# A projection taken two tiles at a time around a chunk batch and the last head's turn, and an output projection whose pools open while retention still holds its own

## The chip, the cores and the metric

The kernel runs on one NeuronCore of a Trainium2 chip. The core's engines run side by side, each in the order its own instruction stream was written in: TensorE (PE in the profile; its weight loads are the row PEld), VectorE (DVE), ScalarE (ACT), GpSimd (POOL) and SyncE (SP), which mostly issues DMAs. A DMA issue that has to wait for its source holds back every later one on the same issuing engine. The metric is device time in microseconds; smaller is better.

## The reference

One layer of a hybrid diffusion backbone over 1024 latent tokens and a 256-token context prefix, width 1024, float32. Cut to what matters here:

```python
p = (h @ w_in)                                    # h: modulated RMSNorm of [context ; latent], 1280 tokens
qkv_a, z, ab, rq, rk, rv, rg = split(p)           # 4 delta-rule heads, 4 retention heads, 128 wide
q, k, v = short_conv(qkv_a)                       # centred, 5 taps, SiLU; q and k are L2-normalised
A   = strict_lower((k*beta) @ k.T * decay)        # per chunk
sol = triangular_solve(A + I, [v*beta, k*beta*exp(G)])
o_gdn = scan over chunks, forward and backward    # state S per head
o_gdn = rms_norm(o_f + o_b) * silu(z)
o_ret = head_group_norm(r_f + r_b) * silu(rg)     # retention, forward and backward
x = x + g1 * (concat(o_gdn, o_ret)[latent] @ w_out)
x = x + g2 * swiglu(modulate(rms_norm(x)), w_ffn_in, w_ffn_out)
return rms_norm(x, final_g)
```

The change touches the z columns of `p`, the building of `A` for the last chunks, and the seam between retention and the product with `w_out`.

## The kernel before, in words

Tokens are taken in ten tiles of 128: tiles 0 and 1 are the context, 2 to 9 the latents. Large products are computed in three fp32r matmuls (high weights by high activations, low by high, high by low), so every weight appears as `whi` and `wlo`, every activation as `hhi` and `hlo`.

Program order around the first part of the change:

- `conv_block` projects one head of q, k or v and convolves it; `vturn(h)` transposes head h of v token by token on TensorE (`vT`, L855), scales it on ScalarE (`vt`, L858) and stores it (L859).
- `pre(t)` prepares tile t for the triangular solve: `kk` (L705), `qt` (L710, its squares summed by ScalarE at L712), `kq` (L715); then for both directions an affine mask on GpSimd (`e`, L722), exponentials on ScalarE (L726), `ut` on VectorE (L730) stored to DRAM as `un` (L734), and `sp` (L733, L737) stored as `sd` (L738).
- The tiles go in three batches, `BATCH = [[0,1,2,9],[3,8,4,7],[5,6]]`, called b0, b1 and b2 below. `invert` solves a batch's 32x32 diagonal blocks on VectorE: it loads them (`X<-un` and `yr<-un`, L753), copies (L756), runs 30 pairs of multiply and subtract (`tmp`, L766; `X`, L770), transposes (`XT`, L774) and stores (`xd`, L776). `merge` puts the blocks together by small matmuls (`m`, L812 to L839), reading `U` and `t` that L788 to L793 load from `un` and `xd`.
- `token_major(g, tiles)` multiplies all tiles by one 256-column group of `w_in`. It takes the tiles in pairs, two PSUM banks at a time; a tile has 24 matmuls (`tm`, L371 to L373), and `tm_store` empties its bank into `res` (for z a SiLU on ScalarE, L532) and stores it (L387). For z, `res` has two buffers. Groups 8 and 9 are z.
- The order written out is: v's convolutions with `vturn(0)` to `vturn(2)`; z's group 8, all eight latent tiles; `vturn(3)`; `pre(5)` and `pre(6)`; `merge(0)`; `invert(1, 2)`, one run of 30 steps over both batches; `merge(1)`, `merge(2)`; z's group 9; then the two-way scan and retention.

Retention's forward pass over the last four tiles is `forward_tail`: transposes of q and k (`rqT`, `rkT`, L1065 and L1066), scores (`rP`, L1079) masked into `pm` (L1081), the output (`ro`, L1088 to L1090), then a group norm (copy `oc` L1092, statistics L1096 and L1098, scaling on ScalarE L1103, gate on GpSimd L1106) and a store to the DRAM tensor `dy` (L1107). The delta rule's half of `dy` is stored by `gate` as `dy<-yo` (L971, L973). After it the pools of retention and scan close, and the output projection begins: `wo_half` prepares half of `w_out` (load `woraw` L1172, high part L1177, low part L1178); `op_y(l)` loads a token tile of `dy` (`yt`), transposes it (`yT`, L1194) and splits it (`yhi` L1197, `ylo` L1198); `op_mm` does the 24 matmuls of one tile and one half of the columns (`op`, L1208 to L1210). The second half of `w_out`'s low and high parts is written partly into the tiles of pool `h2` (`b11`, `t2` and so on), which lies where retention's pool RT lay.

The order of the instructions on each engine isn't that of the source alone: a list scheduler with a simulated timeline picks, at each moment, among the operations whose inputs it expects to be ready, and program order decides between them. Pools matter to it too, since a tile can only be written once the tile that had its space is done with.

Of the kernel before, what the change touches and what calls it, by code (L numbers as in the profile page):

```python
# [8 lines left out]
F32 = mybir.dt.float32  # L9
# [8 lines left out]
P = 128  # L18
# [20 lines left out]
def build(nc, tc, ap, dbg=None, stop=None, marks=None):  # L39
# [151 lines left out]
    try:  # L191
# [187 lines left out]
        def tm_store(g, t, o, finish, store, pl):  # L379
            early = g < 2  # L380
            res = (W2 if early else R1).tile([P, 256], F32, tag="res", name="res", bufs=4 if early else 2)
            finish(t, o[:, 0:256], res)
            if g == 0:
                S.activation(xa[:, t, :], o[:, 256:WIDE], AF.Copy)
            nm, c0 = GROUPS[g // 2], (g % 2) * 256
            dst = zd[t - 2, :, c0:c0 + 256] if nm == "z" else rd[t, :, RD[nm], c0:c0 + 256]
            store.dma_start(dst, res)  # L387

        def token_major(g, tiles, finish, store, pl, q=S):

            w = [tm_weights(g, kh, pl, q) for kh in range(2)]

            for p in range(0, len(tiles), 2):
                pair = [(t, tm_bank(g)) for t in tiles[p:p + 2]]
                for kh in range(2):
                    for t, o in pair:
                        tm_half(o, w[kh], kh, t)
                for t, o in pair:
                    tm_store(g, t, o, finish, store, pl)

        def fin_copy(t, o, res):
# [460 lines left out]
        for h in range(H):  # L862
            vys.append(newy())
            conv_block(8 + h, vys[h], False)
            if h:
                vturn(h - 1, vys[h - 1])
        token_major(8, LAT, fin_gate, S, W)
        vturn(H - 1, vys[H - 1])
        close(CV)
        checkpoint("v")  # L870
        RP = pool("rp", side="right")
        rope = RP.tile([P, TT, P], F32, tag="rope", name="rope")
        GM = pool("gm", side="right")
        for t in BATCH[2]:
            pre(t)
        close(GP)
# [238 lines left out]
        def forward_tail(ts, cur):  # L1115


            nxt = turn(ts[0], True)
            for t in ts:
                kk, vv, gt, qk = nxt  # L1120
                state = cur
                if t < TT - 1:
                    nxt = turn(t + 1, True)
                    cur = rstate(0, kk, vv, cur, "Rf")
                output(t, vv, gt, qk, scores(qk, True), state, True)

        TAIL = 4
        work = [(backward, t) for t in [1, 0] + list(range(TT - 1, 1, -1))] + [(forward, t) for t in range(TT - TAIL)]
        cur = None
        for s, n in enumerate((0,0,3,3,3,2,2,2,1,0)):  # L1130
# [4 lines left out]
            work = work[n:]  # L1135
        forward_tail(range(TT - TAIL, TT), cur)
        checkpoint("scan")
        close(RT)
        close(PK)
        close(SC)  # L1140
        close(RP)
        close(GS)

        H2 = pool("h2")
        X = {n: H2.tile([P, 2, 4, 4, P], F32R, tag=n, name=n) for n in ("b11", "t2", "t1", "t3", "b21", "t4", "b22")}  # L1150

        def xhi(n, q, k=slice(0, 4)):
            return X[n][:, 0, q, k, :]

        def xlo(n, q, k=slice(0, 4)):
            return X[n][:, 1, q, k, :]

        OR = pool("or", side="right")
# [5 lines left out]
        S.dma_start(gain, ap["gains"])  # L1164
        slabs = [X[n][:, i, 3].rearrange("p k t -> p (k t)") for n in X for i in range(2)]

# [13 lines left out]

        wo = [wo_half(n) for n in range(2)]
        dx1 = dr.tile([LT, P, D], F32, tag="dx1", name="dx1")
        SY.dma_start(g1r, grow[0][0].partition_broadcast(P))
        banks(pa=3, pb=2, pc=3)

# [17 lines left out]
        def op_mm(y, n):  # L1203
# [8 lines left out]
            V.tensor_tensor(x1[:, ns], x1[:, ns], xl[:, ns], ALU.add)  # L1212

        held = {}

# [46 lines left out]
        before = None  # L1262
        pairs = (1, 5, 2, 6, 0, 4, 3, 7)
        nxt = op_y(pairs[0])
        for i, l in enumerate(pairs):
            y = nxt
            if l != 7:
                nxt = op_y(pairs[i + 1])
            op_mm(y, int(l == 7))
            if before:  # L1270
# [391 lines left out]
```

## Time and profile before

| what | value |
|---|---|
| time, median of three runs (lowest, highest) | 1473.67 us (1473.1, 1477.56) |
| the profiled execution's own time | 1475.05 us |
| its span, first to last instruction | 1473.3 us |
| mean granted TensorE clock | 0.981 |
| PE busy | 1400.1 us, 95% of the span |
| DVE, ACT, POOL busy | 962.7, 614.1, 592.0 us |
| instructions in the span | 24112 |
| z group 8 to the end of `merge(2)` | 361.6 to about 491 us |
| scan and retention | about 491 to 711 us |
| output projection | from 712.9 us |
| feed-forward | from about 820 us |

TensorE is busy through most of the program. A row of the timeline gives the start, the duration, the engine, the line, the operation with what it writes and reads, and in brackets the idle time ahead of it with what ended it. A view of windows gives each engine's busy time in a stretch, with the clock granted to TensorE and the share of time that the DMA engines were busy.

### The profile page before, as it was taken

Reading aid. Unit: us, or ns where it says so; the run is one execution under the profiler, and the core shown is the slowest. Engines: PE = TensorE matmul, PEld = TensorE weight load, DVE = VectorE, ACT = ScalarE, POOL = GpSimd, SP = SyncE. Lnnn points to the kernel's source line nnn. Section 1 sums busy time; section 2 is a strip of 40 time slices with the busy share of each in tenths; the row PEclk is TensorE's granted clock in tenths of the full one; section 3 lists DMA queues with packets and bytes.
Section 4 is the critical chain, followed back from the end, with each engine's and each line's share of the span. In section 5 each row is a group of like instructions: output and inputs, shape, how many; then the busy total and the mean of one; then the engine's idle time right before and its main releaser. Section 6 shows DMA issues by size and latency. Waiting matters only on the chain.

```text
span 1473.3 us, 24112 instructions
## 1 busy us (share of the span) xinstructions
PE 1400.1 (95%) x8919; PEld 1202.5 (82%) x8919; DVE 962.7 (65%) x1853; ACT 614.1 (42%) x1325; POOL 592.0 (40%) x495
## 2 busy tenths in 40 slices
PE   7999999988879999899799899999999999999997
PEld 2798888978878999898688688877888888788886
DVE  6566789279665344689677877656555564657577
ACT  5553554578522211245443623223333332454445
POOL 0120001144103334244144688898555553335322
PEclk9999999999989999999899999999999999999999
DMA  9536586688797744996533265774222242786863
GB/s 330 190 98 227 175 254 211 196 257 262 224 260 213 286 155 155 414 367 203 191 121 108 91 238 210 248 259 160 103 107 107 107 151 79 239 283 193 296 211 115
DMA packets 170549, 298.14 MB, mean 202 GB/s; under 512 B 43624, under 2 KB 94008, under 8 KB 166080
## 3 DMA queue, kind: packets, MB, share of 16 engines
q1 hardware_dynamic: 118880, 253.17, 50.2%
q10 hardware_dynamic: 49072, 35.83, 7.8%
q0 software_dynamic: 2480, 7.60, 1.4%
q8 instruction: 70, 1.15, 0.3%
q14 instruction: 47, 0.39, 0.1%
HBM read 206.60 MB, written 89.96 MB: 201 GB/s over the span
## 4 chain that ended last, share of the span: by engine, by line
PE 44%; POOL 6%; DVE 3%; DMA 3%; issue 2%; ACT 2%; ACTq 0%; POOLq 0%; DVEq 0%
PE ffn L1351 7%; PE ffn L1350 6%; PE ffn L1349 6%; PE fo L1477 4%; PE fo L1475 4%; PE fo L1476 4%; DMA wd<-tw 2%; PE op L1208 2%; PE op L1209 2%; PE op L1210 2%; POOL ws L1322 1%; POOL tw L1403 1%; POOL tw L1402 1%; POOL tw L1405 1%; PE ru L1032 1%
## 5 line engine op out<-in xcount | busy, mean ns | idle before, releaser
L371 PE MATMUL tm<-whi,hhi 128*128 128x256 f32 (+1 forms) x704 | 201.4, 290 | 11.3 <-ACT res L532 5.3
L372 PE MATMUL tm<-wlo,hhi 128*128 128x256 f32 (+1 forms) x704 | 200.8, 287 | 2.1 <-DVE wlo L345 2.1
L373 PE MATMUL tm<-whi,hlo 128*128 128x256 f32 (+1 forms) x704 | 199.0, 287 | 0.0
L371 PEld LDWEIGHTS tm<-whi,hhi 128*128 128x128 f32 x704 | 134.4, 192 | 14.6 <-ACT res L532 5.7
L372 PEld LDWEIGHTS tm<-wlo,hhi 128*128 128x128 f32 x704 | 135.2, 192 | 4.8 <-DVE wlo L345 2.5
L1349 PE MATMUL ffn<-t,whi 128*128 128x512 f32 x352 | 137.0, 390 | 1.9 <-ACT whi L344 1.9
L1351 PE MATMUL ffn<-t,wlo 128*128 128x512 f32 x352 | 137.0, 390 | 1.2 <-DVE wlo L345 1.2
L1350 PE MATMUL ffn<-t,whi 128*128 128x512 f32 x352 | 137.0, 389 | 0.0
L373 PEld LDWEIGHTS tm<-whi,hlo 128*128 128x128 f32 x704 | 134.4, 192 | 0.8 <-DVE hlo L314 0.2
L344 ACT ACTIVATE whi<-wraw 128x512 fp32r<-128x512 f32 (+2 forms) x98 | 75.2, 771 | 135.7 <-PE ffn L1350 82.7
L344 ACT ACTIVATE whi<-ws 128x512 fp32r<-128x512 f32 x88 | 55.6, 632 | 170.5 <-PE ffn L1350 123.1
L345 DVE TENSOR_TENSOR wlo<-ws,whi 128x512 fp32r<-128x512 f32 x88 | 96.0, 1091 | 44.3 <-ACT whi L344 44.1
L1475 PE MATMUL fo<-whi,ahi 128*128 128x512 f32 x308 | 119.3, 390 | 0.9 <-ACT ahi L344 0.9
L1476 PE MATMUL fo<-wlo,ahi 128*128 128x512 f32 x308 | 120.0, 390 | 0.0
L1477 PE MATMUL fo<-whi,alo 128*128 128x512 f32 x308 | 119.0, 390 | 0.0
L345 DVE TENSOR_TENSOR wlo<-wraw,whi 128x512 fp32r<-128x512 f32 (+2 forms) x92 | 101.7, 1107 | 20.1 <-ACT whi L344 20.0
L1349 PE MATMUL ffn<-b,whi 128*128 128x512 f32 x264 | 103.7, 393 | 4.5 <-ACT whi L344 4.5
L1351 PE MATMUL ffn<-b,wlo 128*128 128x512 f32 x264 | 103.5, 392 | 1.1 <-DVE wlo L345 1.1
L1350 PE MATMUL ffn<-b,whi 128*128 128x512 f32 x264 | 103.4, 392 | 0.0
L611 PE MATMUL b<-hhi,whi 128*128 128x512 f32 (+1 forms) x256 | 95.2, 372 | 0.9 <-ACT y L615 0.9
L613 PE MATMUL b<-hhi,wlo 128*128 128x512 f32 (+1 forms) x256 | 94.8, 370 | 0.0
L612 PE MATMUL b<-hlo,whi 128*128 128x512 f32 (+1 forms) x256 | 94.4, 369 | 0.0
(444 smaller groups left out, 3440.7 us busy)
## 6 DMA issues: line engine op xcount, KB each, us to landing
adaw<-ada SPq DMA_DIRECT2D x48, 512.0 KB, 5.0
pk<-sd SPq DMA_DIRECT2D x16, 1536.0 KB, 13.7
wraw<-wfi SPq DMA_DIRECT2D x44, 512.0 KB, 3.5
ar<-ad SPq DMA_DIRECT2D x33, 512.0 KB, 5.8
w<-wfo SPq DMA_DIRECT2D x22, 512.0 KB, 4.4
wd<-tw SPq DMA_DIRECT2D x11, 1024.0 KB, 4.9
ad<-act SPq DMA_DIRECT2D x20, 512.0 KB, 2.8
raw<-wd SPq DMA_DIRECT2D x20, 512.0 KB, 4.9
```

Of the source, the lines that this page charges most:

```text
L344: S.activation(hi, raw, AF.Copy)
L345: e.tensor_tensor(lo, raw, hi.bitcast(F32), ALU.subtract)
L371: T.matmul(o, hhi[:, k, tsl], whi[:, k % 4, :], start=(k == 0), stop=False)
L372: T.matmul(o, hhi[:, k, tsl], wlo[:, k % 4, :], start=False, stop=False)
L373: T.matmul(o, hlo[:, k, tsl], whi[:, k % 4, :], start=False, stop=(k == KT - 1))
L611: T.matmul(o, whi[:, k, :], hh, start=(k == 0), stop=False)
L1349: T.matmul(o, whi[:, k, :], xhi(xn, slice(0, 4), k), start=(first and k == 0), stop=False, **kw)
L1350: T.matmul(o, whi[:, k, :], xlo(xn, slice(0, 4), k), start=False, stop=False, **kw)
L1351: T.matmul(o, wlo[:, k, :], xhi(xn, slice(0, 4), k), start=False, stop=(k == 3), **kw)
L1475: T.matmul(po[g][i], ahi[:, ts], whi, start=(j == 0 and not kw), stop=False, **kw)
L1476: T.matmul(po[g][i], ahi[:, ts], wlo, start=False, stop=False, **kw)
L1477: T.matmul(po[g][i], alo[:, ts], whi, start=False, stop=(j == FH - 1), **kw)
```

## The change

Every engine keeps its number of instructions; what changes is their order, one buffer count and the order in which pools open and close.

- `res` gets four buffers for every group.
- `token_major` becomes a loop over a generator, `token_pairs`, that yields after each pair of tiles. Group 8 of z now runs thus: `pre(5)` and `pre(6)` first in program order, then two pairs, then `vturn(3)`, then the other two pairs.
- `forward_tail` becomes a generator that yields after each tile. The scan's and retention's other pools close, and the output projection's pools open, ahead of it; retention's pool RT closes behind it. After the tail's first tile come `wo_half(0)` and `op_y` of token tile 1, after its third the first half `op_mm` of that tile. Pool `h2`, the second half of `w_out` and the new PSUM bank tags come after the tail.

```diff
-            res = (W2 if early else R1).tile([P, 256], F32, tag="res", name="res", bufs=4 if early else 2)
+            res = (W2 if early else R1).tile([P, 256], F32, tag="res", name="res", bufs=4)
...
         def token_major(g, tiles, finish, store, pl, q=S):
 
+            for _ in token_pairs(g, tiles, finish, store, pl, q):
+                pass
+
+        def token_pairs(g, tiles, finish, store, pl, q=S):
+
             w = [tm_weights(g, kh, pl, q) for kh in range(2)]
-
             for p in range(0, len(tiles), 2):
                 pair = [(t, tm_bank(g)) for t in tiles[p:p + 2]]
...
                 for t, o in pair:
                     tm_store(g, t, o, finish, store, pl)
+                yield
...
-        token_major(8, LAT, fin_gate, S, W)
+        for t in BATCH[2]:
+            pre(t)
+        z8 = token_pairs(8, LAT, fin_gate, S, W)
+        next(z8)
+        next(z8)
         vturn(H - 1, vys[H - 1])
+        for _ in z8:
+            pass
...
-        for t in BATCH[2]:
-            pre(t)
         close(GP)
...
                 output(t, vv, gt, qk, scores(qk, True), state, True)
+                yield
...
-        forward_tail(range(TT - TAIL, TT), cur)
         checkpoint("scan")
-        close(RT)
         close(PK)
         close(SC)
         close(RP)
         close(GS)
...
-        wo = [wo_half(n) for n in range(2)]
+        wo = []
...
+        pairs = (1, 5, 2, 6, 0, 4, 3, 7)
+        tail = forward_tail(range(TT - TAIL, TT), cur)
+        next(tail)
+        wo.append(wo_half(0))
+        nxt = op_y(pairs[0])
+        next(tail)
+        next(tail)
+        op_mm(nxt, 0)
+        for _ in tail:
+            pass
+        close(RT)
+        H2 = pool("h2")
...
+        slabs = [X[n][:, i, 3].rearrange("p k t -> p (k t)") for n in X for i in range(2)]
+
+        wo.append(wo_half(1))
+        banks(pa=3, pb=2, pc=3)
...
-        pairs = (1, 5, 2, 6, 0, 4, 3, 7)
-        nxt = op_y(pairs[0])
         for i, l in enumerate(pairs):
             y = nxt
             if l != 7:
                 nxt = op_y(pairs[i + 1])
-            op_mm(y, int(l == 7))
+            if i:
+                op_mm(y, int(l == 7))
```

How that moves the instructions is read from the order on an engine. The first place is TensorE at the end of z's group 8, where b2's second tile (6) is prepared. Before, all 192 `tm` matmuls of group 8 come first:

```order
L372 MATMUL tm<-wlo,hhi 128x256
L373 MATMUL tm<-whi,hlo 128x256
L855 MATMUL vT<-ident,y 128x128 x2
L705 MATMUL kk<-kc 128x128 x4
L710 MATMUL qt<-ident,qc 128x128 x2
L855 MATMUL vT<-ident,y 128x128 x4
L710 MATMUL qt<-ident,qc 128x128 x2
L715 MATMUL kq<-qc,kc 128x128 x4
L855 MATMUL vT<-ident,y 128x128 x4
```

In the change the same `kk` and `qt` (now L710 and L715) stand behind 56 of them; `kq` follows 8 `tm` later, and the ten `vT` of the last head after 32 more:

```order
L371 MATMUL tm<-whi,hhi 128x256
L372 MATMUL tm<-wlo,hhi 128x256
L710 MATMUL kk<-kc 128x128 x4
L715 MATMUL qt<-ident,qc 128x128 x4
L373 MATMUL tm<-whi,hlo 128x256
```

So tile 6's preparation moved ahead of 136 `tm` matmuls. On SP, which issues the loads and stores of the solve, the piece from b0's last store on was, before (`un_2892`, `un_2893` and `un_2894` are the `un` of b0, b1 and b2; `xd_3181` is b0's):

```order
L776 DMA xd_3181<-XT 64x1024
L753 DMA X<-un_2893 16x32x32 x4
L734 DMA un_2894<-ut 128x512 x2
L753 DMA yr<-un_2894 8x32x32
L738 DMA sd<-sp 128x1024 x2
L753 DMA X<-un_2894 8x32x32 x4
L753 DMA yr<-un_2894 8x32x32
L788 DMA U_4298<-un_2892 128x4096
L880 DMA rope<-rope 128x1280
L793 DMA t_4300<-xd_3181 32x32x32 x4
```

and is now:

```order
L739 DMA un_2894<-ut 128x512
L758 DMA yr<-un_2894 8x32x32
L743 DMA sd<-sp 128x1024
L781 DMA xd_3181<-X 64x1024
L781 DMA xd_3181<-XT 64x1024
L781 DMA xd_3181<-X 64x1024
L781 DMA xd_3181<-XT 64x1024
L758 DMA X<-un_2893 16x32x32 x4
L793 DMA U_4298<-un_2892 128x4096
L889 DMA rope<-rope 128x1280
L758 DMA X<-un_2894 8x32x32
L798 DMA t_4300<-xd_3181 32x32x32 x4
```

b2's stores of `ut` moved ahead of b0's stores of the solved blocks and of b1's `X` loads. On VectorE the second `ut` of tile 6 likewise stands within the last steps of b0's solve, ahead of `tmp` with 84 columns.

The second place is TensorE at the end of retention. Before, the transposes `yT` come behind the output `ro` of the last tile, and 24 `op` follow:

```order
L1089 MATMUL ro<-Rb_6925,qk 128x128
L1090 MATMUL ro<-vg,pm 128x128
L1088 MATMUL ro<-Rf,qk 128x128
L1089 MATMUL ro<-Rb_6925,qk 128x128
L1090 MATMUL ro<-vg,pm 128x128
L1194 MATMUL yT<-ident,yt 128x128 x8
```

In the change they stand behind `ro` of tile 7, and everything of tiles 8 and 9 from the transposes of q and k on stands behind them, mixed with the 24 `op`:

```order
L1098 MATMUL ro<-Rb_7031,qk 128x128
L1099 MATMUL ro<-vg,pm 128x128
L1186 MATMUL yT<-ident,yt 128x128 x8
L1074 MATMUL rqT<-ident,kq 128x128 x4
L1075 MATMUL rkT<-ident,kq 128x128 x4
L1074 MATMUL rqT<-ident,kq 128x128 x4
L1075 MATMUL rkT<-ident,kq 128x128 x4
L1088 MATMUL rP<-qk 128x128 x4
L1097 MATMUL ro<-Rf,qk 128x128
L1200 MATMUL op<-wohi,yhi 128x512
L1201 MATMUL op<-wolo,yhi 128x512
```

The first `yt` still stands right behind the last `dy<-yo` on SP. Before:

```order
L1172 DMA woraw<-wo 128x512
L664 DMA vg<-rd 128x1024
L1172 DMA woraw<-wo 128x512 x3
L973 DMA dy<-yo 128x512
L664 DMA yt<-dy 128x512 x2
L664 DMA xl<-x 128x1024 x2
```

In the change, where only the loads ahead of it are in another order:

```order
L669 DMA vg<-rd 128x1024
L982 DMA dy<-yo 128x512
L1165 DMA woraw<-wo 128x512 x4
L982 DMA dy<-yo 128x512
L669 DMA yt<-dy 128x512 x2
L669 DMA xl<-x 128x1024 x2
```

From the feed-forward on, the order on TensorE is the same as before.

More of the change, by code (lines that the diff above doesn't have):

```diff
@@ L1142, in build @@
         close(GS)
[L1149 to L1156, printed above, removed]
         OR = pool("or", side="right")
@@ L1164, in build @@
         S.dma_start(gain, ap["gains"])
-        slabs = [X[n][:, i, 3].rearrange("p k t -> p (k t)") for n in X for i in range(2)]
+        slabs = []
         def wo_half(n):
@@ L1179, in wo_half @@
             return hi, lo
-        wo = [wo_half(n) for n in range(2)]
+        wo = []
         dx1 = dr.tile([LT, P, D], F32, tag="dx1", name="dx1")
         SY.dma_start(g1r, grow[0][0].partition_broadcast(P))
-        banks(pa=3, pb=2, pc=3)
         def op_y(l):
@@ L1212, in op_mm, with xhi, xlo @@
             V.tensor_tensor(x1[:, ns], x1[:, ns], xl[:, ns], ALU.add)
+        pairs = (1, 5, 2, 6, 0, 4, 3, 7)
[10 more added lines that the diff above has]
+        H2 = pool("h2")
+        X = {n: H2.tile([P, 2, 4, 4, P], F32R, tag=n, name=n) for n in ("b11", "t2", "t1", "t3", "b21", "t4", "b22")}
+        def xhi(n, q, k=slice(0, 4)):
+            return X[n][:, 0, q, k, :]
+        def xlo(n, q, k=slice(0, 4)):
+            return X[n][:, 1, q, k, :]
+        slabs = [X[n][:, i, 3].rearrange("p k t -> p (k t)") for n in X for i in range(2)]
+        wo.append(wo_half(1))
+        banks(pa=3, pb=2, pc=3)
         held = {}
```

## The prediction, on record before the result was seen

> **What bounds the kernel now.** I read the page's busy times first, then windows cut at the stages the change touches, then TensorE's waits in them, then the timelines of the engines it waits for.
>
> ```profile
> PE 1400.1 (95%) x8919; PEld 1202.5 (82%) x8919; DVE 962.7 (65%) x1853; ACT 614.1 (42%) x1325; POOL 592.0 (40%) x495
> ...
> 360.00:400.00 40.00, 33.10 (x266) 32.69 (x267) 27.86 (x56) 24.62 (x68) 10.26 (x8) 0.96 0.76 211
> 400.00:460.00 60.00, 47.92 (x1019) 45.64 (x1018) 44.46 (x124) 11.08 (x20) 9.71 (x14) 0.88 0.89 249
> 460.00:490.00 30.00, 30.00 (x493) 28.60 (x492) 9.81 (x24) 9.58 (x18) 10.09 (x18) 0.95 0.73 238
> 490.00:580.00 90.00, 90.00 (x795) 89.80 (x794) 36.69 (x118) 10.10 (x15) 37.08 (x77) 1.00 0.49 176
> 580.00:690.00 110.00, 103.81 (x902) 101.71 (x901) 86.86 (x333) 43.65 (x136) 40.32 (x37) 1.00 0.88 336
> 690.00:730.00 40.00, 29.48 (x161) 25.05 (x161) 29.93 (x97) 22.87 (x54) 8.46 (x7) 0.83 0.62 216
> ```
>
> The columns behind the window are its length, the busy time of PE, PEld, DVE, ACT and POOL with counts, TensorE's granted clock and the DMA engines' busy share. TensorE bounds the program. With its instructions unchanged in number, only its idle time and the time that it runs below full clock can change. In the stages touched that is 6.9 us idle in 360 to 400, 12.1 in 400 to 460, 6.2 in 580 to 690 and 10.5 in 690 to 730. From 460 to 580 it never stops, so whatever is saved before 460 is carried into the scan, and 460 to 580 offers nothing itself.
>
> **The z stage: what is removed.** TensorE's waits from 310 to 490 (total, times, longest), and one window:
>
> ```profile
> PE tm L371 <- ACT res L532: 5.3, 2, 4.0
> PE m L819 <- issue: 4.0, 2, 2.2
> PE m L812 <- DMA t<-xd: 3.0, 3, 1.7
> PE m L819 <- DMA U<-xd: 2.5, 1, 2.5
> ...
> 430.00:440.00 10.00, 6.14 (x225) 5.75 (x226) 3.39 (x10) 3.94 (x8) 0.00 (x0) 0.60 0.93 223
> ```
>
> The waits for `t<-xd` and `U<-xd` are merge(0) waiting for the blocks that b0's solve has stored. Why these loads are late stands on SP and VectorE:
>
> ```profile
> 393.62 0.92 SPq L734 DMA_DIRECT2D un<-ut  x2
> 398.98 4.70 SPq L753 DMA_DIRECT2D X<-un  x4
> 406.38 9.89 SPq L793 DMA_DIRECT2D t<-xd  x4
> ...
> 387.86 0.09 DVE L757 MEMSET X<- 128x32 f32 x1 [9.44 <-DMA X<-un]
> 392.90 1.29 DVE L730 SCALAR_TENSOR_TENSOR ut<-kk,e 128x512 f32<-128x512 f32 x2 [0.40 <-PE kk L705]
> 419.50 1.06 DVE L756 COPY X<-yr 32x1024 f32<-32x1024 f32 x1 [5.06 <-DMA yr<-un]
> ```
>
> SP issues in order. b2's `un<-ut` is there only at 393.62, because tile 6's `kk` stood behind all of z's group 8. Its loads follow, and b0's `t<-xd` stand behind them, from 406.38. With tile 6's `kk` behind 56 of the 192 `tm`, I estimate it at about 368.4, its stores done some 12 us earlier, and `t<-xd` issued from about 394. Removed then: 3.0 and 2.5 of waits; the longer of the two waits "issue" of L819 (2.2), which lies in the slice of clock 0.60; what this slow clock costs, 0.40 x 6.14 = 2.5; a further 1.3 of what the rest of 400 to 460 loses to its clock (0.12 x 47.92 = 5.8 in all); and, with four `res` buffers, the shorter wait for `res`, 5.3 - 4.0 = 1.3. Sum 12.8 us. The 5.06 us of VectorE for b2's `yr` also go, off TensorE's path.
>
> **What it adds there.** Tile 6's exponentials come to ScalarE among z's SiLUs, each change of function with a table load:
>
> ```profile
> 376.38 1.28 ACT L726 ACT_TABLE_LOAD   x1
> 377.67 1.28 ACT L726 ACTIVATE e<-e,nG 128x128 f32<-128x128 f32 x4
> 379.48 1.28 ACT L532 ACT_TABLE_LOAD   x1
> 380.78 0.66 ACT L532 ACTIVATE res<-tm 128x256 f32<-128x256 f32 x2
> ```
>
> These rows are the longest wait for `res` (4.0 us): the SiLU that empties a bank stands behind a table load, four exponentials and a second table load. In the change tile 6's four squares join that queue, and it is now the first group of `vT` and the `tm` behind it that wait. I take 5.4 us for it, +1.4. Bounds are 0 and one more round of table load and exponentials (1.28 + 1.28 + 1.28 = 3.8). The queue behind that SiLU holds `vt` of the last head, which nothing needs before the scan.
>
> A second price lies on VectorE: the second `ut` of tile 6 stands within b0's last steps and waits for its mask and exponentials, about 379.8 by the rows above. b0's stores follow it, then b1's `X` loads. I estimate b1's first step at 394.4 instead of 387.86, 6.5 us later; the 5.06 us that b2 no longer costs give most of it back. The 37 `tm` of the next part, which now stand ahead of the merges' end, cover the rest, so I price it at 0 on TensorE's path; its cover gone, it costs 6.5.
>
> The sum is -12.8 + 1.4 = -11.4; I take **-10**, since the DMA engines stay near full there (0.89 over 400 to 460). Ends: -13, and -2 if the loads land hardly sooner.
>
> **The scan.** By the order, TensorE does 37 more `tm` before the last `merge` is over. At the 0.113 us of a matmul in 490 to 580 (90.00 by 795) that is 4.2 us, so as much less is left to fill the scan, and the 6.2 us idle of 580 to 690 may grow by at most that. Bounds 0 and +4.2; I take **+1**, as TensorE is full for 120 us ahead of it.
>
> **The tail.** Rows of TensorE, then of SP, VectorE, ScalarE and the landing time of `yt`:
>
> ```profile
> 693.65 0.39 PE L1090 MATMUL ro<-vg,pm 128*128 128x128 f32 x2
> ...
> 694.88 1.06 PE L1079 MATMUL rP<-qk 128*128 128x128 f32 x8
> 697.85 1.16 PE L1079 MATMUL rP<-qk 128*128 128x128 f32 x8 [1.34 <-ACT qk L1068]
> 701.28 0.49 PE L1088 MATMUL ro<-Rf,qk 128*128 128x128 f32 x2 [2.27 <-DVE Rf L1038]
> 703.71 0.80 PE L1090 MATMUL ro<-vg,pm 128*128 128x128 f32 x2 [1.51 <-DVE pm L1081]
> 709.86 0.39 PE L1088 MATMUL ro<-Rf,qk 128*128 128x128 f32 x2
> 710.30 0.39 PE L1090 MATMUL ro<-vg,pm 128*128 128x128 f32 x2
> 710.52 1.04 PE L1194 MATMUL yT<-ident,yt 128*128 128x128 f32 x8
> 718.88 0.39 PE L1208 MATMUL op<-wohi,yhi 128*128 128x512 f32 x1
> 720.03 0.39 PE L1210 MATMUL op<-wohi,ylo 128*128 128x512 f32 x1
> 726.59 0.78 PE L1208 MATMUL op<-b,yhi 128*128 128x512 f32 x1
> ...
> 703.08 0.33 SPq L973 DMA_DIRECT2D dy<-yo  x1
> 703.46 0.92 SPq L664 DMA_DIRECT2D yt<-dy  x2
> ...
> 701.93 1.12 DVE L971 SCALAR_TENSOR_TENSOR yo<-O,rgy,zg 128x128 f32<-128x128 f32 x4
> ...
> 721.59 1.65 ACT L1103 ACTIVATE oc<-oc,nm,rry 128x128 f32<-128x128 f32 x4 [2.01 <-DVE nm L1101]
> ...
> DMA to landing us min/median/max: 3.8/4.6/5.4
> ```
>
> Before, TensorE reaches the last tiles early and picks up their pieces as they come; `yt` (issued 703.46, with 4.3 us between bounds of 3.8 and 5.4 it is there at 707.8) is needed only at 710.52, so it costs nothing. In the change `yT` stands ahead of all of tiles 8 and 9, and `yt` is still behind the last `dy<-yo` on SP. That one waits for the gate's `yo`, 701.93 to 703.05, whose place in VectorE's order is the same (842 of its rows stand ahead in both). So TensorE, done with tile 7 at 693.9, waits for `yt` until about 707.8.
>
> Then it has, without a stop: 8 `yT` 0.9; two `rP` 2.0 (each 8 passes in 1.06); 16 transposes at a little under that pass's 0.13, 1.8; 24 `ro` at 0.22 (709.86 to 710.30 is two steps), 5.3; 24 `op` at 0.23 (five steps from 718.88 to 720.03), 5.6. That is 15.6, so the last `ro` ends at 723.4. The `op` with `b` can only start once RT is free, which takes the last tile's norm: from the scaling at 721.59 to the `op<-b` at 726.59 it is 5.0, and copy, statistics and root ahead of it I estimate at 3.7 from their rows. That makes 732.1 against 726.59, +5.5, with 24 `op` and 24 `yT` done by then in both. Two `qk` now stand behind `yo` on VectorE, which may bring it forward a little, so I take **+4**. Ends: -3, if `yt` lands near 700 (17 us of TensorE's work then cover the norm), and +8, if the gate slips by 2.5 us.
>
> ```profile
> 704.29 0.63 PE L1088 MATMUL ro<-Rf,qk 128*128 128x128 f32 x2
> 706.85 0.63 PE L1088 MATMUL ro<-Rf,qk 128*128 128x128 f32 x2
> ```
>
> Here six `ro` take 2.56 us, 0.43 each instead of 0.22: full speed was withdrawn after waits of 1.3, 2.3 and 1.5 us. The Trainium skill ("TensorE: Matmul & The Clock Gate", "What's actually happening" in Part 1) says that a window of about 3.4 us idle halves the clock and that 3.4 us of work restore it. By it one wait of 13 us costs a single slow stretch, an estimate of 1.7 us by that page, where the rows of before show about 3.2 (3.4 us here, 3.0 near 716, half of each lost), so the sum would be 1.5 lower. The trace agrees on the length of the slow stretch and not on the idle needed. I leave it out of the sum.
>
> **Sum.** -10 + 1 + 4 = -5 on the profiled execution's own 1475.05, which is 1.4 above the median of the runs shown: 1470.05 there, 1468.7 on the median's footing.
>
> **Rivals.** (1) The tail gains too. The 24 `op` fill TensorE while retention's pieces are late, as the 10.5 us idle in 690 to 730 invite. For it: VectorE is busy 29.93 of 40 there, so an earlier `yo` is possible once the program ahead is shorter. Against it: `yt` is behind `dy<-yo` in both orders. With the tail at -3: -10 + 1 - 3 = -12, 1461.7.
> (2) The preparation doesn't come through: tile 6's `kk` is early, but with DMA near full the blocks land hardly sooner, and merge(0) still waits. The z stage gives -3 and tail and scan take +4 and +1: +2, 1475.7. For it speaks 0.93 in the slow slice; against it, that b2's stores went out as soon as tile 6's `ut` was there (392.90 and 393.62), not when the DMA engines had room.
> (3) Slower: b1's solve becomes the chain. It starts 6.5 us later, since b0's stores now stand behind tile 6's `ut`. From the point where b1's stored blocks land after TensorE has reached merge(1), the cover is gone: 6.5 comes onto the path, and only merge(0)'s waits and the short `res` wait are saved (3.0 + 2.5 + 1.3 = 6.8). With +1.4, +1 and the tail's full +5.5: +7.6, 1481.3. For it: b1 has twice the blocks of b2, and DVE is busy 44.46 of 60 in 400 to 460. Against it: 84 `tm` of z's group 9 and b0's merge lie between.
>
> **How the numbers follow.** Less than 0.3%, 4.4 us, can't be told from no change here. The forecast has 0.45; its own range, 1463 to 1474, puts 0.28 of that beyond the 4.4 us on the fast side and 0.17 within. Rival 1 has 0.20, all faster; rival 2 0.17, 0.11 within and 0.06 slower; rival 3 0.18, all slower. Faster 0.48, same 0.28, slower 0.24. The range, from a little beyond rival 1 to most of rival 3, is 1459 to 1480.5.
>
> **What would show it.** Right on the z stage: `t<-xd` issued near 394 instead of 406.38, no wait at merge(0)'s first matmuls, a clock above 0.85 where 0.60 stood, a wait for `res` of 5 us behind `vT`, and b1's first step near 394. Right on the tail: one wait of 10 us or more ahead of `yT` in place of 1.3, 2.3 and 1.5, ended by the DMA of `yt`, and `op<-b` some 38 us behind the end of tile 7's `ro` instead of 32.7. Wrong: `yt` landing before TensorE is done with tile 7, merge(1) waiting for b1's blocks, or idle in 580 to 690 above 10 us.

## The result, and the profile after

The change makes the kernel slower: 1490.49 us median (1484.18 to 1492.84, four runs) against 1474.79 (1473.1 to 1477.56, four runs), a ratio of 1.0104 with a 95% interval of 1.0083 to 1.0124. That is 15.3 us lost where 5 us of gain were forecast, and above the range. The profiled execution of the change has a span of 1491.0 us, 17.7 more than the one of before.

The windows of the change, with the columns as before (length, then PE, PEld, DVE, ACT and POOL busy, clock, DMA share):

```profile
360.00:400.00 40.00, 33.26 (x260) 31.95 (x259) 25.25 (x49) 24.32 (x68) 12.71 (x9) 0.96 0.91 272
400.00:460.00 60.00, 47.10 (x709) 44.72 (x708) 37.23 (x110) 10.88 (x20) 4.34 (x7) 0.86 0.75 201
430.00:440.00 10.00, 10.00 (x90) 9.58 (x90) 4.95 (x12) 2.78 (x4) 0.00 (x0) 0.81 0.30 86
450.00:460.00 10.00, 7.62 (x44) 7.41 (x45) 2.19 (x8) 0.00 (x0) 0.00 (x0) 0.66 0.82 196
580.00:690.00 110.00, 103.40 (x895) 101.07 (x894) 85.79 (x323) 40.49 (x121) 37.46 (x38) 1.00 0.88 333
690.00:730.00 40.00, 28.02 (x176) 25.26 (x175) 27.06 (x89) 19.56 (x53) 9.16 (x8) 0.83 0.62 216
730.00:745.00 15.00, 8.69 (x49) 7.11 (x49) 8.33 (x31) 7.89 (x17) 2.53 (x2) 0.75 0.38 127
```

By the clock on the wall little differs until 690. The order of work was changed, though, so the same moment does not hold the same work. I therefore compared the time at which TensorE had done equal amounts of work: each matmul counted by its usual step (0.117 us for a `tm`, 0.23 for a 512-column matmul, 0.0105 for a 32x32 `m`, 0.112 for the others). This is my own working from the traces; other weights for the small matmuls move a time by up to 2 us and the differences by about 1. Between the amounts that the kernel before had done at two moments:

| stretch (of before) | before | change |
|---|---|---|
| 360 to 500: z, solve, merges | 140.7 us | 145.9 us |
| 500 to 580: projections | 80.0 | 80.0 |
| 580 to 735: scan, retention, the seam | 154.9 | 165.4 |
| 735 to 830: output projection | 94.9 | 95.2 |

Two places lose, 5 us and 10.5 us. The first is a single execution against a single execution. The four kernels below that change only the tail, and so keep TensorE's order of before in this stage but for some small merge matmuls, took 137.1 to 140.1 us in their profiles. Two more with the change's order there took 141.1 (the z stage alone) and about 144 (the change with its tail mended). The two sets don't overlap, which speaks for a loss of a few us in this stage.

The z stage. TensorE's waits from 310 to 503 in the change:

```profile
PE tm L371 <- ACT res L537: 5.4, 2, 3.8
PE m L817 <- DMA t<-xd: 5.1, 1, 5.1
PE vT L860 <- ACT res L537: 4.2, 1, 4.2
PE m L827 <- issue: 3.5, 2, 2.6
PE kk L710 <- issue: 3.0, 1, 3.0
...
PE tm L372 <- issue: 1.9, 1, 1.9
PE tm L371 <- issue: 1.3, 1, 1.3
```

(total us, times, longest us.) And the rows of SP, VectorE, ScalarE and TensorE behind them:

```profile
394.87 10.50 SPq L798 DMA_DIRECT2D t<-xd  x4
...
395.25 0.09 DVE L762 MEMSET X<- 128x32 f32 x1 [10.24 <-DMA X<-un]
418.59 0.69 DVE L820 COPY xt<-m 128x512 f32<-128x512 f32 x1 [7.60 <-PE m L817]
438.37 1.13 DVE L779 COPY XT<-X 128x1024 f32<-128x1024 f32 x1
...
412.21 0.38 ACT L537 ACTIVATE res<-tm 128x256 f32<-128x256 f32 x1 [7.75 <-DMA yr<-un]
...
412.65 0.39 PE L371 MATMUL tm<-whi,hhi 128*128 128x256 f32 x1 [3.81 <-ACT res L537]
452.38 0.28 PE L817 MATMUL m<-t,U 32*32 32x32 f32 x2 [5.11 <-DMA t<-xd]
```

b0's `t<-xd` is issued at 394.87 as forecast (394), and merge(0) no longer waits for it. In its place TensorE waits 3.8 us for a SiLU; ScalarE had stood 7.75 us, by the profile until a load of b2's blocks had ended. VectorE, whose next instruction is merge(0)'s copy `xt`, stands 7.6 us for TensorE within b1's solve, and so b1's last step (`XT`) comes 43 us behind its first where before it was 36 (387.86 to 424.18):

```profile
424.18 1.12 DVE L774 COPY XT<-X 128x1024 f32<-128x1024 f32 x1
```

merge(1) then waits 5.1 us for b1's blocks.

The tail, TensorE and then SP:

```profile
696.31 1.90 PE L1088 MATMUL rP<-qk 128*128 128x128 f32 x8 [3.01 <-ACT qk L1077]
704.77 0.39 PE L1099 MATMUL ro<-vg,pm 128*128 128x128 f32 x2
711.85 1.09 PE L1186 MATMUL yT<-ident,yt 128*128 128x128 f32 x4 [6.68 <-DMA yt<-dy]
714.58 1.09 PE L1186 MATMUL yT<-ident,yt 128*128 128x128 f32 x4 [1.65 <-DMA yt<-dy]
736.80 0.63 PE L1186 MATMUL yT<-ident,yt 128*128 128x128 f32 x4 [2.44 <-DVE ylo L1190]
739.12 1.09 PE L1186 MATMUL yT<-ident,yt 128*128 128x128 f32 x4 [1.69 <-DMA yt<-dy]
742.04 0.80 PE L1200 MATMUL op<-b,yhi 128*128 128x512 f32 x1 [1.84 <-ACT b L1170]
...
708.38 0.33 SPq L982 DMA_DIRECT2D dy<-yo  x1
708.75 1.00 SPq L669 DMA_DIRECT2D yt<-dy  x2
```

`yt` is issued right behind the last `dy<-yo`, and TensorE waits for it twice. Then, from the last `ro` (it ends near 733.5) to `op<-b` at 742.04, it waits again. Both are the forecast's picture, though I had put down one wait of 10 us or more where there are two, of 6.7 and 1.7; the sizes are taken up below. TensorE is done with tile 7's `ro` at 705.2 here, 11.1 us later than before, so most of the loss is there ahead of `yT`. That doesn't make the tail cheap: the last `dy<-yo` is late as well, 708.38 against 698.61 in the tail-only run below.

### The profile page after: what moved, and what is told of

It reads as the page before. It is cut to its first block, busy times and chain, and to the rows that moved or that the text cites. A ratio compares the mean times of both kernels' runs of the same rounds, so it can differ in the third digit from the quotient of the medians.

```text
span 1491.0 us, 24119 instructions
## 1 busy us (share of the span) xinstructions
PE 1406.7 (94%) x8919; PEld 1206.9 (81%) x8919; DVE 957.7 (64%) x1853; ACT 613.5 (41%) x1325; POOL 590.4 (40%) x495
## 4 chain that ended last, share of the span: by engine, by line
PE 40%; POOL 6%; DMA 2%; issue 1%; DVE 1%; ACT 0%; SPq 0%; POOLq 0%; ACTq 0%
PE ffn L1366 6%; PE ffn L1365 6%; PE ffn L1364 6%; PE fo L1492 5%; PE fo L1490 5%; PE fo L1491 5%; PE op L1200 2%; PE op L1202 2%; PE op L1201 2%; DMA wd<-tw 2%; POOL tw L1418 1%; POOL ws L1337 1%; POOL tw L1420 1%; POOL tw L1417 1%; POOL tw L1419 1%
## 5 line engine op out<-in xcount | busy, mean ns | idle before, releaser
L1366 PE MATMUL ffn<-t,wlo 128*128 128x512 f32 x352 | 137.1, 390 | 1.4 <-DVE wlo L345 1.4
L345 DVE TENSOR_TENSOR wlo<-ws,whi 128x512 fp32r<-128x512 f32 x88 | 91.9, 1046 | 47.8 <-ACT whi L344 47.7
L617 PE MATMUL b<-hlo,whi 128*128 128x512 f32 (+1 forms) x256 | 94.9, 371 | 0.0
```

What stands on the lines that cost most here:

```text
L345: e.tensor_tensor(lo, raw, hi.bitcast(F32), ALU.subtract)
L1366: T.matmul(o, wlo[:, k, :], xhi(xn, slice(0, 4), k), start=False, stop=(k == 3), **kw)
```

## The experiments

All ratios are against the kernel before on the same chip, with 95% intervals; microseconds beside them are the ratio's excess over 1 times about 1475 us. The diffs are against the kernel before, unless they say otherwise.

**One part at a time.** The z stage alone (the change's hunks up to `close(GP)`, of which these two set the order):

```diff
-        token_major(8, LAT, fin_gate, S, W)
+        for t in BATCH[2]:
+            pre(t)
+        z8 = token_pairs(8, LAT, fin_gate, S, W)
+        next(z8)
+        next(z8)
         vturn(H - 1, vys[H - 1])
+        for _ in z8:
+            pass
...
-        for t in BATCH[2]:
-            pre(t)
```

> Only the z stage of the change: four res buffers, pre(5) and pre(6) ahead of group 8 of z, that group in pairs around the last head's turn; tail as before. My theory after the result is that the parts add up: from the lag of TensorE at equal work (1.8 us at 360, about 7 at 500, 7.6 at 680) the z stage alone costs 5 to 8 us, so 1.0035 to 1.0055 of before. The rival says that the lag that arises before 500 is the spread of an execution (a slow start of kk at 338, issue waits) and the z stage as such is worth 0 or a gain as predicted: 0.993 to 1.001. In the trace: b0's stores held until tile 6's ut is done (380), b1's first step near 395, a wait of 5 us for t<-xd at merge(1).

Measured: 1.0047 (1.0024 to 1.007), 6.9 us. Its profiled execution, the slowest of its five, doesn't place this loss: at equal work it is only 2.1 us behind the one of before over 360 to 500 and 580 to 735 together, and some 7 of its 10 us are lost behind 780 us, where TensorE's order is that of before. The tail alone (the hunks from `forward_tail` on):

> Only the tail of the change: pools of the output projection opened ahead of the tail, its half of w_out, yT of tile 1 and 24 op within the tail; z stage as before. Theory: TensorE waits for yt with everything of tiles 8 and 9 behind it, and the tail alone costs 9 to 11 us, 1.006 to 1.0075 of before, with one wait of 6 us or more ahead of yT and op<-b about 41 us behind the end of tile 7's ro instead of 32.7. Rival: most of the 10 us is what the shorter filler of the scan hands on, and the tail alone costs 4 us or less (1.003 or less).

Measured: 1.0077 (1.0056 to 1.0098), 11.4 us. The two sum to 1.0124, and the whole is 1.0104: the parts add within their intervals. Its tail, three windows and three rows of TensorE:

```profile
690.00:702.00 12.00, 0.81 (x8) 0.62 (x6) 10.59 (x43) 6.58 (x14) 1.93 (x2) 0.71 0.79 259
702.00:710.00 8.00, 5.04 (x20) 3.88 (x21) 4.19 (x12) 5.51 (x13) 3.31 (x3) 0.50 0.84 297
710.00:720.00 10.00, 10.00 (x60) 9.08 (x59) 1.38 (x2) 1.79 (x3) 1.72 (x2) 0.90 0.16 55
...
702.26 1.12 PE L1177 MATMUL yT<-ident,yt 128*128 128x128 f32 x4 [11.45 <-DMA yt<-dy]
724.52 0.39 PE L1090 MATMUL ro<-vg,pm 128*128 128x128 f32 x2
733.45 0.79 PE L1191 MATMUL op<-b,yhi 128*128 128x512 f32 x1 [1.88 <-ACT b L1161]
```

Here the wait for `yt` stands in one piece, 11.45 us, and TensorE then works at half clock for the 8 us to 710, and by the next window for some 2 us more.

**Which piece of the tail.** The pools opened early, `op_y` and its 24 `op` behind the last tile (against the tail alone):

```diff
         next(tail)
         wo.append(wo_half(0))
-        nxt = op_y(pairs[0])
-        next(tail)
-        next(tail)
-        op_mm(nxt, 0)
         for _ in tail:
             pass
+        nxt = op_y(pairs[0])
+        op_mm(nxt, 0)
```

> The tail with its pools opened early and half of w_out prepared within it, as in the change, but op_y of tile 1 and its 24 op in program order behind the last tile, still ahead of the closing of pool RT; z stage as before. On TensorE yT then stands behind the last ro, as before. Theory: what costs is yT ahead of tiles 8 and 9, so this is within 2 us of before (0.9985 to 1.0015). Rival: what costs is the opening of the pools ahead (other buffers, other waits), so this loses the same 9 to 11 us as the tail alone (1.006 to 1.0075).

Measured: 1.002 (1.0005 to 1.0034), 2.9 us. Most of the loss lies in the place of `yT` and `op`; opening the pools early has a small price of its own, 0.7 to 5 us by the interval.

Why is `yt` behind the last `dy<-yo` at all? Its rows of `dy` are written earlier. But pool OY now opens on space that the scan's pools held until their last tile was done with. So the next kernel gives tile 1's `yt` a space of its own (against the tail alone):

```diff
-                yt = load(OY, dy[l, :, half * 512:half * 512 + 512], "yt", 2, (P, 512))
+                if l == pairs[0]:
+                    yt = load(RT, dy[l, :, half * 512:half * 512 + 512], "yt0", 2, (P, 512))
+                else:
+                    yt = load(OY, dy[l, :, half * 512:half * 512 + 512], "yt", 2, (P, 512))
```

> The tail alone as in the tail-only run, but the two yt of tile 1 lie in retention's pool RT instead of in pool OY, whose space the scan's pools held until now; z stage as before. Theory: yt stands behind the last dy<-yo because its space is one that the scan frees last, not because its data is late. With a space of its own its issue moves ahead of the last two dy<-yo on SP, yT needs no wait, and the 9 to 11 us of the tail go: 0.996 to 1.002. Rival: the rows of dy are late as well (or DMA at 0.9 and VectorE's backlog bound the tail), so TensorE still stalls and it stays at 1.005 or more.

Measured: 1.0051 (1.0035 to 1.0068), 7.5 us. SP and TensorE:

```profile
685.64 0.80 SPq L664 DMA_DIRECT2D yt<-dy  x2
693.97 8.33 SPq L973 DMA_DIRECT2D dy<-yo  x2
...
722.23 0.39 PE L1090 MATMUL ro<-vg,pm 128*128 128x128 f32 x2
725.91 1.28 PE L1180 MATMUL yT<-ident,yt 128*128 128x128 f32 x8 [2.42 <-DVE ylo L1184]
730.64 0.80 PE L1194 MATMUL op<-b,yhi 128*128 128x512 f32 x1 [3.45 <-ACT b L1161]
```

Half of my theory holds: `yt` now goes out at 685.64, ahead of the last two `dy<-yo`, and the wait for it is gone. The other half falls: only some 4 us come back, and the intervals overlap. TensorE is done with the last `ro` at 722.6 and has nothing but transposes until 730.64. The 24 `op` that stood there before, as cover for the last tile's norm, have been done. So the next kernel puts other work there: token tile 5's transposes and first 24 `op` (against the kernel with `yt` in its own space):

```diff
         for _ in tail:
             pass
+        y2 = op_y(pairs[1])
+        op_mm(y2, 0)
         close(RT)
...
-            if l != 7:
+            if not i:
+                nxt = y2
+            elif l != 7:
                 nxt = op_y(pairs[i + 1])
-            if i:
+            if i > 1:
                 op_mm(y, int(l == 7))
```

> The tail with yt of tile 1 in its own space, as in that run, and also the next token tile's (5) transposes and first 24 op placed behind the last tile, ahead of the closing of RT, so that TensorE has 22 op (5.1 us at 0.23) between the last ro and op<-b. Theory: with yt in time, what is left of the tail's loss (5 to 7 us at equal work) is that the 24 op that covered the last tile's norm now stand ahead of it, so TensorE waits through the norm. With new cover 4 to 5 us come back against that run: 1.0005 to 1.003. Rival: the loss lies ahead of the last ro (ScalarE and VectorE work of yhi, ylo between the tail's steps), the cover is worth nothing, and it stays at 1.004 to 1.006.

Measured: 0.9995 (0.998 to 1.001). From the last `ro` to `op<-b` TensorE's longest wait is now 0.69 us:

```profile
719.55 0.39 PE L1090 MATMUL ro<-vg,pm 128*128 128x128 f32 x2
723.36 0.50 PE L1194 MATMUL op<-wohi,yhi 128*128 128x512 f32 x1 [0.69 <-ACT yhi L1183]
727.28 0.71 PE L1194 MATMUL op<-b,yhi 128*128 128x512 f32 x2
```

With both mended, `yt` late for want of space and the norm bare of cover, the tail is level with before; it doesn't gain. The cover without a space of its own for `yt` was not run, so how the loss divides between the two is known only in this order: some 4 us, then some 8.

**Which piece of the z stage.** Early `pre`, with group 8 in one piece and the turn behind it:

```diff
+        for t in BATCH[2]:
+            pre(t)
         token_major(8, LAT, fin_gate, S, W)
         vturn(H - 1, vys[H - 1])
...
-        for t in BATCH[2]:
-            pre(t)
```

> z stage: four res buffers and pre(5), pre(6) ahead of group 8 of z in program order, but the group undivided and the last head's turn behind it, as before; tail as before. If the early preparation of tile 6 is what delays b0's stores and b1's solve, this loses what the z stage loses, 5 to 8 us (1.0035 to 1.0055). If instead the turn of the last head in the middle of the group (its vT behind a SiLU, its vt ahead of the next SiLU on ScalarE) is what costs, this is at before's time or better (0.996 to 1.001).

Measured: 0.9998 (0.9981 to 1.0014). The turn in the middle, `pre` late as before:

> z stage: four res buffers and the last head's turn in the middle of group 8, but pre(5), pre(6) behind the group in program order as before; tail as before. If the turn's place by itself costs the 6 us, 1.003 to 1.005. If it costs only together with the early preparation (tile 6's exponentials and the turn meeting on ScalarE), 0.999 to 1.001.

Measured: 1.001 (0.9987 to 1.0033). Neither has a loss of its own that shows, though the second interval leaves room for up to 4.9 us and overlaps the z-only run's. TensorE's waits from 360 to 503 with early `pre` in one piece:

```profile
PE m L812 <- DMA t<-xd: 6.3, 1, 6.3
PE m L819 <- issue: 4.8, 1, 4.8
```

Both are longer than in the change (5.1 and 3.5), in a kernel that is level with before. So neither wait makes a loss by itself. Both kernels have four `res` buffers, and so I ran that edit alone:

> Only res with four buffers for every group, all else as before. By the prediction's term, 1.3 us of waiting for res go: 0.999. If the wider pool moves other tiles and so other waits, up to 0.2% either way; at 0.999 to 1.001 it is no part of the loss.

Measured: 1.0023 (1.0006 to 1.004), 3.4 us lost, where 1.3 of gain were expected. This edit is not the buffer count alone: with it the scheduler chose another order for TensorE from about 417 us on, and 360 to 500 took 5 to 8 us more than before in its profile (the slowest of its ten runs), as much as in the change or more. A reordering that nobody asked for can thus be worth as much as the loss in question. The counterpart, the z stage with two buffers:

> The z stage as in the z-only run with res left at two buffers. If the wider res is what costs (four buffers alone gave 1.0023), this is 0.2% better than the z-only run's 1.0047: 1.0015 to 1.003. If the order of pre and turn is what costs, it is the same or worse, as SiLUs wait for stores again: 1.0045 to 1.007.

Measured: 1.0073 (1.0046 to 1.0099). This interval overlaps the z-only run's (1.0024 to 1.007), so it isn't shown that the four buffers help there; that they are what costs is not borne out, since without them nothing came back. Then I tried to take away, one at a time, the waits that the trace of the change names. The stores of z issued by GpSimd, so that no store can hold ScalarE (against the z-only kernel):

```diff
-        z8 = token_pairs(8, LAT, fin_gate, S, W)
+        z8 = token_pairs(8, LAT, fin_gate, G, W)
...
-        token_major(9, LAT, fin_gate, S, W)
+        token_major(9, LAT, fin_gate, G, W)
```

> The z stage as in the z-only run, but z's stores (groups 8 and 9) are issued by GpSimd instead of ScalarE; tail as before. Theory: in the change a 128 KB store's issue on ScalarE waited 7.8 us behind b2's block loads and held the next SiLU, on which TensorE waited 3.8 us. With the stores elsewhere the waits of TensorE for res (7.9 us after 370 in the change) shrink to 3 or less, and the z stage loses 0 to 3 us instead of 6.9: 1.000 to 1.002. Rival: what costs is b1's solve (t<-xd 5 us at merge(1)) and the shorter filler in the scan, and it stays at 1.0035 or more.

Measured: 1.004 (1.0027 to 1.0052). The theory falls, since TensorE still waits for the SiLUs:

```profile
PE tm L371 <- ACT res L537: 7.2, 3, 5.6
PE m L827 <- issue: 5.0, 2, 2.7
PE m L817 <- DMA t<-xd: 3.6, 2, 3.3
```

The same edit to the kernel before:

> The kernel before with z's stores issued by GpSimd instead of ScalarE. The wait for res before is 5.3 us in two pieces; if the store issues on ScalarE are part of it, 0.997 to 0.999, faster than both kernels; if the SiLU behind table loads and exponentials is all of it, 0.999 to 1.001.

Measured: 1.0017 (1.0002 to 1.0032): not faster. Next, `xt` moved from VectorE to ScalarE, to take the 7.6 us hold out of b1's solve (against the z-only kernel):

```diff
-            V.tensor_copy(xt1.rearrange("p n j -> p (n j)")[:, :nu * 32], ps1[:, :nu * 32])
+            S.activation(xt1.rearrange("p n j -> p (n j)")[:, :nu * 32], ps1[:, :nu * 32], AF.Copy)
...
-                V.tensor_copy(xt2.rearrange("p n j -> p (n j)"), ps1)
+                S.activation(xt2.rearrange("p n j -> p (n j)"), ps1, AF.Copy)
```

> The z stage as in the z-only run (four res, early pre, turn in the middle; tail as before), with merge's copies xt from PSUM done by ScalarE instead of VectorE. Theory: in the change merge(0)'s first xt stands within b1's solve on VectorE and holds it for 7.6 us, because TensorE is late with merge(0) (it waits for a SiLU); b1's blocks are then late and merge(1) waits 5 us. With xt off VectorE that hold goes: b1's last step comes 5 us or more earlier against its first step, the wait for t<-xd at merge(1) falls below 1 us, and the stage gains 4 to 6 us against the z-only run's 1.0047: 1.0005 to 1.002. Rival: the wait at merge(1) only moves (to res, or to the scan), and it stays at 1.0035 or more.

Measured: 1.0022 (1.0005 to 1.0039). Its control, the same edit to the kernel before:

> The kernel before with merge's copies xt on ScalarE: the control for the run with xt moved in the z stage. Before, VectorE waits for merge's m once for 6.3 us, behind b2's and ahead of nothing that TensorE waits for, so 0.998 to 1.001. If it gains as much as the z stage does, the hold is no matter of the change.

Measured: 1.0002 (0.9984 to 1.002). The 1.0022 lies between what the two theories said, and its interval overlaps the z-only run's. The trace speaks against the mechanism: the hold by `xt` is gone, and VectorE waits for other things instead, so that b1's last step is where it was in the z-only run (434.04 here, 433.56 there). TensorE's wait for b1's blocks went only from 4.6 to 3.3 us, not below 1. VectorE's waits in 386 to 450 and that step:

```profile
DVE wlo L345 <- ACT whi L344: 5.8, 2, 5.4
DVE X L761 <- DMA zd<-res: 4.8, 1, 4.8
...
434.04 1.04 DVE L779 COPY XT<-X 128x1024 f32<-128x1024 f32 x1
```

Last, the ten `vt` of the last head scaled by VectorE instead of ScalarE (against the z-only kernel):

```diff
-                    S.activation(vt[:, t], ps[:, t * P:(t + 1) * P], AF.Copy, scale=sv3[:, t0 + t, h:h + 1])
+                    if h == H - 1:
+                        V.tensor_scalar(vt[:, t], ps[:, t * P:(t + 1) * P], sv3[:, t0 + t, h:h + 1], None, ALU.mult)
+                    else:
+                        S.activation(vt[:, t], ps[:, t * P:(t + 1) * P], AF.Copy, scale=sv3[:, t0 + t, h:h + 1])
```

> The z stage as in the z-only run with the last head's ten vt scaled by VectorE (idle there for 10 us, waiting for b1's blocks) instead of ScalarE. Theory: early pre and the middle turn cost only together (0.9998 and 1.001 apart, 1.0047 together), because the exponentials and the vt then both stand ahead of z's SiLUs on ScalarE. With vt off ScalarE (2.7 us of it) the waits for res shrink and it comes to 1.000 to 1.002. Rival: ScalarE's place in it is small, b1's late solve and a scan with less filler carry the loss, and it stays at 1.0035 or more.

Measured: 1.0029 (1.001 to 1.0049), between the two expectations again, and TensorE's waits for `res` are little changed (3.9 and 3.8 us in all, 2.7 and 3.7 in the z-only run). Two things weaken this run as a test: with the edit the scheduler gave TensorE another order in this stage, and the profiled execution was the fastest of its ten (1475.04 us, the median is 1478.34). In that execution the waits for `res` are all there, and it is no slower than the one of before. In none of the three runs did the wait of TensorE that the edit was aimed at go away, and each one's interval overlaps the z-only run's. What carries the z stage's loss isn't shown by them.

**Together.** Early `pre` in one piece, with the mended tail:

> Early pre with the group undivided (0.9998 by itself) together with the tail whose yt has its own space and which has 24 more op behind the last tile (0.9995 by itself). If the parts add, 0.998 to 1.001; if the scan's share that each moves is the same idle time, 1.001 or more.

Measured: 1.0002 (0.9983 to 1.0021). The same early `pre` with only `yt` in its own space, run earlier:

> Both parts without what the theory blames: pre(5), pre(6) ahead of an undivided group 8 with the turn behind it, four res buffers, and the tail with yt of tile 1 in RT. If the parts add, it is the sum of the pre-first run (0.9998) and of yt in its own space: 0.995 to 1.002. A loss of over 0.3% would say that the theory names the wrong pieces.

Measured: 1.0022 (1.0002 to 1.0042), a little beyond what was expected; the two parts by themselves sum to 1.0049, and the intervals still overlap. The whole change with the mended tail (`yt` in its own space, and cover):

> The whole change with the tail's two repairs: yt of tile 1 in its own space, and tile 5's transposes and first 24 op behind the last tile. If the tail's share of the loss is what the repairs took back in the tail-only runs (1.0077 to 0.9995) and the z stage's share is unchanged, this is at the z-only run's time: 1.003 to 1.006. If the shares interact, it is 1.007 or more, or 1.001 or less.

Measured: 1.0028 (1.0011 to 1.0046): of 1.0104 three quarters are gone, and a z share of 4.1 us (1.6 to 6.8) is left. With `xt` and `vt` moved as well:

> As before it, and with merge's xt on ScalarE and the last head's vt on VectorE. If these two repairs take back 0.0025 each in the z stage, 0.998 to 1.001. If they do the same thing twice, 1.001 to 1.004.

Measured: 1.0044 (1.0026 to 1.0061). The two edits that seemed to take back a little each do not do so together, which is one more reason not to read their single results as repairs; with `vt` moved the scheduler's order is another one here too. No kernel was faster than the one before by more than its interval.

## Why the prediction was wrong

The chance went 0.48 to faster and 0.24 to slower, and the time lies 10 us beyond the range. By its own steps:

**The z stage's removals: right for the blocks, and worth nothing.** I forecast `t<-xd` near 394 (394.87), b1's first step near 394 (395.25), no wait at merge(0)'s first matmuls (none for a DMA), and a wait for `res` of about 5 us at the middle turn (4.2). These came where I placed them. The clock did not: I forecast above 0.85 where 0.60 had stood, and 430 to 440 has 0.81, 450 to 460, around the new wait at merge(1), 0.66. The step that failed is the sum, "-12.8 + 1.4": it took the old waits away and priced the new order's waits only where I had looked, at the one SiLU and at b1's start. Of the 12.8 us only the 5.5 of merge(0)'s waits for `t<-xd` and `U<-xd` went. The change has three waits in the stage that stand in the sum at nothing: 3.8 us for a SiLU just where merge(0) had waited for its blocks, 5.1 us for b1's blocks at merge(1), and 6.7 us by "issue" from 361 on (3.5 + 1.9 + 1.3) where before had 4.9 (4.0, and 0.9 in the line below) and I had taken 2.2 off.

```profile
PE tm L371 <- issue: 0.9, 1, 0.9
```

The clock stayed as low (0.86 over 400 to 460, 0.88 before), so the 3.8 us that I took for it were not there either. Alone, the stage's edit costs 6.9 us (3.5 to 10.3) instead of gaining 10.

**b1's late solve: seen, and covered by the wrong thing.** I had it start 6.5 us late and priced it at 0, because 37 `tm` stood ahead of the merges' end. It did start late, by 7.4. But the 37 are no cover for merge(1) if TensorE's order puts merge(1)'s matmuls where they must wait; they did, for 5.1 us. That was rival 3's mechanism, which I gave 0.18. The runs don't confirm it as the cause, though: with the hold on b1's solve removed the loss was not clearly smaller, and early `pre` in one piece is level with before in spite of a longer wait for `t<-xd`, 6.3 us. Nor do they rule it out, since no run took the wait at merge(1) away. What carries the z stage's loss stays open. Shown is only that early `pre` by itself is level with before, that the turn in the middle by itself has no loss that shows, that together they cost 3.5 to 10 us, and that none of three edits aimed at single waits clearly brings this back. That it is the order the scheduler makes of the edit, and not the edit as such, is a rival that no run tests.

**The scan: about as priced.** From 580 to 735 the z-only kernel needed 156.6 us at equal work, 1.7 more than before; I took +1, with bounds of 0 and 4.2.

**The tail: right in kind, too small by more than half.** The wait for `yt` is there, ended by its DMA, 11.45 us in the tail-only run where I worked out 13.9. The way from the last `ro` to `op<-b` is 8.5 us there (724.9 to 733.45), where I had 8.7. The term that was mis-sized is "without a stop", 15.6 us from `yT` to the last `ro`. Measured: 702.26 to 724.9, 22.6 us. Of the 7.0 too much, 3.0 are waits of that chain (0.31 for the second `yt`, 1.21 and 1.17 for `ylo`, 0.34 for `pm`) and about 3.5 are the clock: 2.5 in 702 to 710 (5.04 us of work at 0.50) and 1.0 in 710 to 720 (10.00 us at 0.90). The remaining 0.5 us I have not placed.

In the change itself `op<-b` comes 36.9 us behind the end of tile 7's `ro` (705.16 to 742.04), close to the 38 that I gave as a sign. That is luck, since two errors cancel: the wait ahead of `yT` is 6.7 us instead of 13.9, as TensorE gets there late, and from `yT` to the last `ro` it takes 21.6 instead of 15.6.

That clock is the point at which I weighed the Trainium skill against the trace ("TensorE: Matmul & The Clock Gate", Part 1) and left it out of the sum. That page of the Trainium skill says that an idle window of about 3.4 us halves the clock; after 11.45 us of idling the profile grants 0.50, which agrees. By the same part of the Trainium skill full clock is back after one such window of work, and I took before's own slow stretches to be as dear. The slow stretch in the tail-only run lasted not 3.4 but about 10 us from `yT` on: 0.50 over 702 to 710, and 0.90 over 710 to 720, which is 2 us more at 0.50. TensorE worked only 5.04 of the first 8 us, in pieces; whether that is the reason, no run tests. My reading of before was short too. I read 3.4 us of slow `ro`, but the window around them has 0.66, which is 6.8 us at 0.50:

```profile
700.00:710.00 10.00, 7.22 (x40) 6.92 (x41) 7.94 (x35) 3.03 (x6) 0.00 (x0) 0.66 0.76 266
```

On top, I chose +4 where the sum gave +5.5. The measured price of the tail alone is 11.4 us (8.3 to 14.5), above my upper end of 8.

**The rivals.** Rival 1 (the tail gains) had "an earlier `yo`" as its condition. The run with `yt` in its own space shows that the condition was the wrong one: with `yt` in time the tail still lost 7.5 us. I had written, as a good sign, that 17 us of TensorE's work would then cover the norm; in fact that work stood ahead of the norm and covered nothing.

## What to carry to other kernels

Work that is moved forward to fill a stall leaves the place it came from, so ask first what it was covering there: here 24 matmuls left the drain of the last tile's norm bare, and putting other matmuls there was worth some 8 us. When a pool opens on space that another stage still holds, look at the loads into it: here `yt` took its place behind that stage's last release, however early its data was. And a sum of removed waits is at best an upper bound: here merge(0)'s waits for its blocks went as counted, others stood in their place, and such waits must be looked for at every point where two engines meet. Where a scheduler makes the order, an edit is not one change: compare the orders that came out before the times are read as the edit's price.

## What the runs showed of the hardware that was not expected

- TensorE is held by "issue" (it waits for nothing that the profile shows) near the bursts of 32x32 matmuls in the merges, in every one of these kernels, for amounts that differ: 4.0 us at `m` in the kernel before, 3.5 in the change, 4.8 with early `pre` in one piece, 0.9 with the tail alone, 6.6 in the kernel before with z's stores on GpSimd.
- After a wait of 11.45 us the granted clock was 0.50 over the following 8 us, in which TensorE was busy for 5.04.
- One order of instructions is not one time within a stage: over 360 to 500 five kernels with the order of before took 137.1 to 140.7 us at equal work in their profiled executions, and three with the change's order 141.1, about 144 and 145.9. A difference of 3 us between two single profiles of this stage says nothing by itself.
